# Side-by-side substitution for the latents' triangular inverses in a DeltaNet and PEER kernel

## The chip, the cores and the metric

One core of one Trainium2 chip. The metric is the device time of one execution in microseconds (us); lower is better. Engines: PE (TensorE), DVE (VectorE), ACT (ScalarE), POOL (GpSimd), SP (which here only issues DMAs).

## The reference, cut to what matters

One DeltaNet layer over 512 latent tokens, seeded by scans over 256 context tokens, then a PEER expert layer. The part that the change touches is the inverse of a unit lower-triangular matrix per chunk, head and direction:

```python
def _unit_lower_inverse(a):
    """(I + a)^-1 for strictly lower-triangular a (..., C, C), C = 2^DN_CHUNK_LOG2."""
    eye = jnp.eye(a.shape[-1], dtype=a.dtype)
    t = eye - a
    p = a
    for _ in range(DN_CHUNK_LOG2 - 1):
        p = p @ p
        t = t @ (eye + p)
    return t
...
    a = jnp.where(strict, jnp.einsum('bhnid,bhnjd->bhnij', kb, k) * dmat, 0.0)
    t = _unit_lower_inverse(a)
    u = t @ (v * beta[..., None])
    w = t @ (kb * jnp.exp(G)[..., None])
```

The kernel works with chunks of 128 tokens instead of 64, which gives the same scan. The latents then have 4 chunks x 8 heads = 32 matrices of 128 x 128 for each of two directions (the set N[0], in the trace Nf, is upper-triangular in memory, the set N[1], Nb, lower). The context has 32 matrices for both directions together (Nc).

## The kernel before

**Rounds.** `Trunk.run` is written as rounds t = 1 to 50 (the loop `for t in range(1, nj + 3)`). Round t does one step of several jobs: the projection of job t (`Pj`, 24 matmuls of 512 columns, L333, into one of two PSUM buffers "pz"), the convolution taps of job t-1 (one ACT copy, L346, and four dependent DVE instructions, L353, which free the pz), copies to tokens for job t-2 (L758), the split of the weight block for job t+2 into a high part on ACT (L325) and a low part "wl" on POOL (L326), and the load of a weight block on SP's queue. Jobs 0 to 31 are the context's and the latents' q and k; jobs 32 to 47 are alternately values ("v") and gates ("g") in the order `vgvvgggvvgvggvvg`. A gate job has no taps: its pz is freed by ACT. Two raw weight blocks and three split ones are held at a time.

**The inverse.** A set of 32 matrices is inverted in blocks of 32 x 32: `inv_blocks` copies the diagonal blocks together (L433), transposes them on DVE (L445, L447), clears the result V on POOL (L451 to L453), and then runs 31 steps of forward substitution. Step p is, for each set, a multiplication (L459) of column p of A with row p of V into a scratch tile invT, and a subtraction (L462) of that from the rows below p. Each has (31-p)(p+1) elements per partition. Both run on DVE: `PI` and `PS`, which could send some to POOL, are empty. For the latents the two sets alternate: multiply set 0, multiply set 1, subtract set 0, subtract set 1, so that neighbours never depend on each other. For the context there is one set, and each instruction needs the one before. `inv_merge` then transposes and copies on DVE (L473, L433) and joins the blocks by small matmuls (L487) with ACT copies between them (L501 to L539).

**What orders the work.** The inverses are Python generators; `fill` advances one by so many yields at fixed places of a round. The latents' generator starts at the end of round 33 (one yield), gets four yields in each of rounds 34 to 48, and what is left in round 49. The two constants `SL = (50, 2)` are its last round and the steps per slice: after every two steps `inv_blocks` yields twice. The set-up takes 10 yields, the 31 steps 30, and the merges of both sets 32. The program order so made is a priority: the instruction order on each engine is fixed at build time from it and from when operands are expected to be ready, and an engine then runs its list strictly in order. In rounds 41 to 48, DVE also has four multiplications per round with the adaLN weights (L203, tile adaw).

**Memory.** Each of the latents' sets has a work tile of 4096 floats per partition (A, V, and UT, whose start serves as Cc for the first copies): set 0 in pool `tp` (tag big), set 1 in pool `ux`, whose space was the context's until its scans ended. invT is 256 floats with two buffers.

After the rounds, the latents' scan (L550, L558 and others) needs both inverted sets, and everything behind it (output projection, queries, experts) follows the scan.

Of the kernel before, what the change touches and what calls it, by code (L numbers as in the profile page):

```python
# [9 lines left out]
F32 = mybir.dt.float32  # L10
# [5 lines left out]
OP = mybir.AluOpType  # L16
# [4 lines left out]
P = 128  # L21
# [41 lines left out]
MODS = ((25, 2, 0, 8), (41, 4, 16, 8))  # L63
MO = (48, 64)
SC = (17, 28, 2)
SL = (50, 2)
SCAN0 = 25
HOLD = 3
MK = (6, 2)
# [10 lines left out]
HP = dict(taps=0, silu=0, split=0, copies=0, c=0, l=0)  # L80
ALD = "aAaAaaAaAaaAAAaA"
WOV = (3, 4, 5, 6)
PI = (0, 0)
PS = (0, 0)
CONSTS = ("ident", "le", "ge", "ones", "iota", "half")
CONSTS_R = ("gt", "lt", "ident", "negf", "negb")

# [24 lines left out]
class Trunk:  # L112
# [308 lines left out]

    def inv_work(self, N, nf, pool):
        ws = pool.tile([P, 4096], F32, name="inv", tag="big", bufs=1)
        A, V = (ws[:, i * 1024:(i + 1) * 1024].rearrange("p (a b) -> p a b", b=32) for i in range(2))
        UT = ws[:, 2048:4096].rearrange("p (k x) -> p k x", x=64)
        Cc = ws[:, 2048:3072].rearrange("p (x k) -> p x k", k=32)
        return N, nf, A, V, UT, Cc, self.tp.tile([P, 256], F32, name="invT", bufs=2)

    def cp(self, i, nf, b, dst, src):
        nc, e = self.nc, CP[i][nf // 16][b]
        nc.scalar.copy(dst, src) if e == "a" else (nc.vector if e == "v" else nc.gpsimd).tensor_copy(dst, src)  # L433

    def inv_blocks(self, sets, per):
        nc, half = self.nc, self.C["half"]
        swap = lambda z: z.rearrange("p i x -> p x i")
        for N, nf, A, V, UT, Cc, T_ in sets:
            for b in range(4):
                r = blk(b)  # L440
                self.cp(0, nf, b, Cc[r], N[r, :, r].rearrange("p k x -> p x k"))
                if len(sets) > 1:
                    yield
            if nf:
                nc.vector.transpose(A, Cc)  # L445
            if nf < 32:
                nc.vector.transpose(swap(V if nf else A), Cc)  # L447
            if 0 < nf < 32:
                nc.vector.tensor_scalar(A, A, half[:, 0:1], None, op0=OP.mult)
                nc.vector.scalar_tensor_tensor(A, V, half[:, 1:2], A, op0=OP.mult, op1=OP.add)  # L450
            nc.gpsimd.memset(V, 0.0)  # L451
            nc.gpsimd.memset(V.rearrange("p a b -> p (a b)")[:, 0:1024:33], 1.0)
            nc.gpsimd.memset(UT, 0.0)  # L453
            yield
        for p in range(31):
            n = 31 - p
            ms = [T_[:, :n * (p + 1)].rearrange("p (j c) -> p j c", c=p + 1) for *_, T_ in sets]
            for i, (m, (N, nf, A, V, *_)) in enumerate(zip(ms, sets)):
                (nc.gpsimd if i and PI[0] <= p < PI[1] else nc.vector).tensor_tensor(m, A[:, p + 1:, p:p + 1].to_broadcast([P, n, p + 1]),  # L459
                                        V[:, p:p + 1, :p + 1].to_broadcast([P, n, p + 1]), op=OP.mult)  # L460
            for i, (m, (N, nf, A, V, *_)) in enumerate(zip(ms, sets)):
                (nc.gpsimd if i and PS[0] <= p < PS[1] else nc.vector).tensor_tensor(V[:, p + 1:, :p + 1], V[:, p + 1:, :p + 1], m, op=OP.subtract)  # L462
            if p % per == per - 1:
                yield
                yield

    def inv_merge(self, N, nf, A, V, UT, Cc, T_):
        nc = self.nc
        W = A
        swap = lambda z: z.rearrange("p i x -> p x i")  # L470
# [46 lines left out]
        for l2 in (0, 16):  # L517
            W2s, ps = [], []
            for lo in (l2, l2 + 8):
                s, d = (0, 1) if up(lo) else (1, 0)  # L520
# [82 lines left out]
    def run(self):  # L603
        nc, a, C, mod, ng, dram, tc = self.nc, self.a, self.C, self.mod, self.ng, self.dram, self.tc
        with ExitStack() as tk:
# [247 lines left out]
            mq, mk, live, sums, sqs = [], [], [], [], []  # L853

            def inv_c():
                w = self.inv_work(Nc, 16, self.tp)
                yield from self.inv_blocks([w], SC[2])
                yield from self.inv_merge(*w)

            def inv_l():  # L860
                w = [self.inv_work(N[0], 32, self.tp), self.inv_work(N[1], 0, ux)]
                yield from self.inv_blocks(w, SL[1])
                g = [self.inv_merge(*x) for x in w]
                while g:
                    u = g.pop(0)
# [899 lines left out]
```

## Time and profile before

| what | us |
|---|---|
| median of 3 runs | 1951.41 |
| lowest and highest run | 1949.15, 1956.68 |
| time of the profiled execution | 1956.64 |
| its span in the profile | 1954.9 |
| PE busy | 1819.3 (93%) |
| DVE busy | 1562.8 (80%) |
| POOL busy | 625.6 (32%) |

All trace rows come from the one profiled execution; the time around its span is 1956.64 - 1954.9 = 1.74 us. A timeline row gives start and duration in us; where an instruction had to wait after it was issued, its duration includes the wait, and the bracket at the end says how long the engine was idle before it and for whom.

### The profile page before, as it was taken

What the parts mean: (1) busy time and instruction counts of PE and PEld (TensorE: products, weight loads), DVE (VectorE), ACT (ScalarE), POOL (GpSimd) and SP (SyncE); (2) the same over time, 40 slices, a digit from 0 to 9 for tenths busy, and PEclk for the clock granted to TensorE, in tenths of its full rate; (3) what the DMA queues carried; (4) which work ended last, traced back from release to release, by engine and by line L of the source; (5) the groups of instructions that cost most, each with busy time, mean ns of one, the idle gap of its engine ahead of it and who ended that gap; (6) DMA issues with size and microseconds to landing.
All of it is one profiled execution on the core that took longest, in us unless ns stands there. A gap on an engine that the chain in (4) does not pass through costs nothing.

```text
span 1954.9 us, 29971 instructions
## 1 busy us (share of the span) xinstructions
PE 1819.3 (93%) x11119; PEld 1609.9 (82%) x11119; DVE 1562.8 (80%) x3267; ACT 855.1 (44%) x1399; POOL 625.6 (32%) x395
## 2 busy tenths in 40 slices
PE   7778899878998899799999999999999999999997
PEld 4776788766898887689999888788999998889996
DVE  5998967979388789978999687777777887777885
ACT  3655634523445243247666533333333333333333
POOL 1544412361001133321111022333444443434433
PEclk8888879988799899899999999999999999999998
DMA  8221346424635532147999989999989988989981
GB/s 307 67 87 54 87 130 207 133 86 146 190 114 179 177 98 87 55 162 265 308 316 316 327 292 321 323 346 323 314 311 326 334 304 311 328 304 318 325 275 64
DMA packets 202274, 440.65 MB, mean 225 GB/s; under 512 B 15504, under 2 KB 103696, under 8 KB 198800
## 3 DMA queue, kind: packets, MB, share of 16 engines
q1 hardware_dynamic: 155472, 269.87, 42.5%
q0 software_dynamic: 36864, 134.23, 19.4%
q10 hardware_dynamic: 9792, 34.64, 4.4%
q8 instruction: 87, 1.43, 0.3%
q14 instruction: 59, 0.48, 0.1%
HBM read 388.88 MB, written 49.81 MB: 224 GB/s over the span
## 4 chain that ended last, share of the span: by engine, by line
PE 51%; DVE 11%; DMA 5%; issue 1%; SPq 1%; ACT 0%; DVEq 0%; ACTq 0%
PE pz L1232 25%; PE y L1574 21%; PE py L1509 2%; DMA hTt<-hT_d 2%; DMA ge<-pre_d 2%; DVE wk L1350 1%; PE pz L333 1%; DVE keys L1353 1%; DVE keys L1352 1%; DVE row L1288 1%; DVE keys L1349 1%; DVE keys L1351 1%; DVE wl L1603 1%; DMA keys<-G_d 0%; PE pk L1106 0%
## 5 line engine op out<-in xcount | busy, mean ns | idle before, releaser
L1232 PE MATMUL pz<-hH,wh 128*128 128x384 f32 (+1 forms) x1128 | 391.6, 347 | 2.5 <-ACT small L1253 2.5
L1232 PE MATMUL pz<-hH,wl 128*128 128x384 f32 (+1 forms) x1128 | 389.2, 345 | 0.0
L1232 PE MATMUL pz<-hL,wh 128*128 128x384 f32 (+1 forms) x1128 | 388.8, 345 | 0.0
L1280 POOL DMA_INDIRECT row<-u,small x128 | 169.0, 1320 | 478.3 <-DVE row L1288 456.1
L1597 ACT CAST wh<-w 128x1024 fp32r<-128x1024 f32 x196 | 205.4, 1054 | 181.7 <-PE y L1574 98.0
L1603 DVE TENSOR_TENSOR wl<-w,wh 128x1024 fp32r<-128x1024 f32 x196 | 240.4, 1227 | 46.5 <-ACT wh L1597 46.3
L1280 POOL DMA_INDIRECT row<-v,small x128 | 180.2, 1408 | 223.1 <-DVE small L1296 204.8
L326 POOL TENSOR_TENSOR wl<-w,wh 128x1024 fp32r<-128x1024 f32 x53 | 149.0, 2814 | 294.6 <-ACT wh L325 291.2
L1574 PE MATMUL y<-wh,ch 128*128 128x512 f32 x768 | 238.6, 392 | 2.8 <-ACT ch L1560 2.8
L1574 PE MATMUL y<-wh,cl 128*128 128x512 f32 x768 | 238.0, 391 | 1.8 <-DVE cl L1561 1.8
L1574 PE MATMUL y<-wl,ch 128*128 128x512 f32 x768 | 237.7, 391 | 0.0
L1232 PEld LDWEIGHTS pz<-hH,wh 128*128 128x128 f32 x1128 | 213.6, 189 | 9.5 <-ACT small L1253 2.9
L1232 PEld LDWEIGHTS pz<-hL,wh 128*128 128x128 f32 x1128 | 213.4, 189 | 6.4 <-issue 0.2
L1232 PEld LDWEIGHTS pz<-hH,wl 128*128 128x128 f32 x1128 | 213.2, 189 | 4.3
L1574 PEld LDWEIGHTS y<-wh,cl 128*128 128x128 f32 x768 | 144.2, 188 | 33.4 <-DVE cl L1561 2.8
L1574 PEld LDWEIGHTS y<-wl,ch 128*128 128x128 f32 x768 | 144.5, 188 | 31.4
L1574 PEld LDWEIGHTS y<-wh,ch 128*128 128x128 f32 x768 | 143.5, 188 | 28.9 <-ACT ch L1560 3.5
L1296 DVE SCALAR_TENSOR_TENSOR small<-row,small 128x1024 f32<-128x1024 f32 x127 | 162.6, 1280 | 1.2
L1288 DVE SCALAR_TENSOR_TENSOR row<-row,small 128x1024 f32<-128x1024 f32 x128 | 155.2, 1219 | 0.0
L1253 ACT ACTIVATE ge<-pz 128x384 f32<-128x384 f32 x108 | 53.5, 495 | 214.1 <-PE pz L1232 212.8
L333 PE MATMUL pz<-hlH,wh 128*128 128x512 f32 x256 | 112.4, 439 | 24.4 <-DVE acc L353 19.8
L1516 ACT ACTIVATE keys<-py 128x512 f32<-128x512 f32 x96 | 105.0, 1093 | 55.7 <-PE py L1509 50.8
(477 smaller groups left out, 3361.0 us busy)
## 6 DMA issues: line engine op xcount, KB each, us to landing
w<-uT SPq DMA_DIRECT2D x128, 512.0 KB, 5.0
w<-v SPq DMA_DIRECT2D x128, 512.0 KB, 5.1
w<-w_in SPq DMA_DIRECT2D x48, 512.0 KB, 3.7
G_d<-keys ACTq DMA_DIRECT2D x24, 1024.0 KB, 6.5
adaw<-adaT SPq DMA_DIRECT2D x64, 256.0 KB, 3.4
keys<-G_d SPq DMA_DIRECT2D x8, 1536.0 KB, 13.5
Gt<-G_d SPq DMA_DIRECT2D x8, 1536.0 KB, 13.8
w<-w_q SPq DMA_DIRECT2D x16, 512.0 KB, 3.7
```

Of the source, the lines that this page charges most:

```text
L326: self.last_split = (eng or nc.gpsimd).tensor_tensor(wl, w, wh.bitcast(F32), op=OP.subtract)
L333: self.nc.tensor.matmul(z[:, :T], w_[c // 4][:, c % 4, :] if isinstance(w_, list) else w_[:, c, :], src[x_][:, c, :], start=c + n == 0, st ...
L1232: self.nc.tensor.matmul(out, w[i][:, c, :], x_[:, c, sl], start=c == 0 and n == 0, stop=c == NC - 1 and n == 2)
L1253: self.nc.scalar.activation(ge, z, AF.Gelu)
L1280: nc.gpsimd.indirect_dma_start(out=r, out_offset=None, in_=a["u"] if k < P else a["v"], in_offset=bass.IndirectOffsetOnAxis(ap=self.idx[:, ...
L1288: nc.vector.scalar_tensor_tensor(r, r, 1.0, self.xg, op0=OP.mult, op1=OP.mult, accum_out=self.hid_g[:, k:k + 1])
L1296: nc.vector.scalar_tensor_tensor(self.yg, r, self.coef[:, k:k + 1], self.yg, op0=OP.mult, op1=OP.add)
L1509: nc.tensor.matmul(gp[:, r * P:(r + 1) * P], e[:, 2 + r // 2, :, r % 2], oa[:, 2 * w + r // 2, :, r % 2], start=r == 0 and w == 0, stop=w ...
L1516: nc.scalar.activation(Gs[:, :, i * 4:i * 4 + 4].rearrange("p a t -> p t a"), gps.pop(p).rearrange("p (t a) -> p t a", t=4), AF.Copy, scal ...
L1574: nc.tensor.matmul(yp[2 * t + hf], c_[:, t * P:(t + 1) * P], v_[:, hf * 512:hf * 512 + 512], start=b == 0 and w == 0, stop=b == NBLK - 1 a ...
L1597: nc.scalar.copy(wh, w)
L1603: nc.vector.tensor_tensor(wl, w, wh.bitcast(F32), op=OP.subtract)
```

## The change

The two sets of the latents get one common tile for A and V (in pool `ux`), arranged so that A of set 0 and A of set 1 lie one behind the other, and so do the two V; both UT share the tile in `tp`. One multiplication and one subtraction per step then cover both sets, with twice the elements: 62 instructions for the 31 steps in place of 124. invT becomes one buffer of 2 x 256. The context's inverse goes through the same code with one set. A slice has three steps in place of two, so the 31 steps take 20 yields in place of 30. The constants `PI` and `PS`, which chose no step, go.

```diff
--- before.py
+++ after.py
@@ -63,7 +63,7 @@
 MODS = ((25, 2, 0, 8), (41, 4, 16, 8))
 MO = (48, 64)
 SC = (17, 28, 2)
-SL = (50, 2)
+SL = (50, 3)
 SCAN0 = 25
 HOLD = 3
 MK = (6, 2)
@@ -80,8 +80,6 @@
 HP = dict(taps=0, silu=0, split=0, copies=0, c=0, l=0)
 ALD = "aAaAaaAaAaaAAAaA"
 WOV = (3, 4, 5, 6)
-PI = (0, 0)
-PS = (0, 0)
 CONSTS = ("ident", "le", "ge", "ones", "iota", "half")
 CONSTS_R = ("gt", "lt", "ident", "negf", "negb")
 
@@ -421,21 +419,25 @@
 
 
 
-    def inv_work(self, N, nf, pool):
-        ws = pool.tile([P, 4096], F32, name="inv", tag="big", bufs=1)
-        A, V = (ws[:, i * 1024:(i + 1) * 1024].rearrange("p (a b) -> p a b", b=32) for i in range(2))
-        UT = ws[:, 2048:4096].rearrange("p (k x) -> p k x", x=64)
-        Cc = ws[:, 2048:3072].rearrange("p (x k) -> p x k", k=32)
-        return N, nf, A, V, UT, Cc, self.tp.tile([P, 256], F32, name="invT", bufs=2)
+    def inv_work(self, sets, av, uts):
+        n = len(sets)
+        AV = av[:, :2048 * n].rearrange("p (q s a b) -> p q s a b", q=2, s=n, b=32)
+        T_ = self.tp.tile([P, 2, 256], F32, name="invT", bufs=1)[:, :n]
+        w = []
+        for i, (N, nf) in enumerate(sets):
+            ut = uts[:, i * 2048:i * 2048 + 2048]
+            w.append((N, nf, AV[:, 0, i], AV[:, 1, i], ut.rearrange("p (k x) -> p k x", x=64),
+                      ut[:, :1024].rearrange("p (x k) -> p x k", k=32)))
+        return w, AV[:, 0], AV[:, 1], T_
 
     def cp(self, i, nf, b, dst, src):
         nc, e = self.nc, CP[i][nf // 16][b]
         nc.scalar.copy(dst, src) if e == "a" else (nc.vector if e == "v" else nc.gpsimd).tensor_copy(dst, src)
 
-    def inv_blocks(self, sets, per):
+    def inv_blocks(self, sets, As, Vs, T_, per):
         nc, half = self.nc, self.C["half"]
         swap = lambda z: z.rearrange("p i x -> p x i")
-        for N, nf, A, V, UT, Cc, T_ in sets:
+        for N, nf, A, V, UT, Cc in sets:
             for b in range(4):
                 r = blk(b)
                 self.cp(0, nf, b, Cc[r], N[r, :, r].rearrange("p k x -> p x k"))
@@ -454,17 +456,15 @@
             yield
         for p in range(31):
             n = 31 - p
-            ms = [T_[:, :n * (p + 1)].rearrange("p (j c) -> p j c", c=p + 1) for *_, T_ in sets]
-            for i, (m, (N, nf, A, V, *_)) in enumerate(zip(ms, sets)):
-                (nc.gpsimd if i and PI[0] <= p < PI[1] else nc.vector).tensor_tensor(m, A[:, p + 1:, p:p + 1].to_broadcast([P, n, p + 1]),
-                                        V[:, p:p + 1, :p + 1].to_broadcast([P, n, p + 1]), op=OP.mult)
-            for i, (m, (N, nf, A, V, *_)) in enumerate(zip(ms, sets)):
-                (nc.gpsimd if i and PS[0] <= p < PS[1] else nc.vector).tensor_tensor(V[:, p + 1:, :p + 1], V[:, p + 1:, :p + 1], m, op=OP.subtract)
+            sh = [P, len(sets), n, p + 1]
+            m = T_[:, :, :n * (p + 1)].rearrange("p s (j c) -> p s j c", c=p + 1)
+            nc.vector.tensor_tensor(m, As[:, :, p + 1:, p:p + 1].to_broadcast(sh), Vs[:, :, p:p + 1, :p + 1].to_broadcast(sh), op=OP.mult)
+            nc.vector.tensor_tensor(Vs[:, :, p + 1:, :p + 1], Vs[:, :, p + 1:, :p + 1], m, op=OP.subtract)
             if p % per == per - 1:
                 yield
                 yield
 
-    def inv_merge(self, N, nf, A, V, UT, Cc, T_):
+    def inv_merge(self, N, nf, A, V, UT, Cc):
         nc = self.nc
         W = A
         swap = lambda z: z.rearrange("p i x -> p x i")
@@ -853,13 +853,15 @@
             mq, mk, live, sums, sqs = [], [], [], [], []
 
             def inv_c():
-                w = self.inv_work(Nc, 16, self.tp)
-                yield from self.inv_blocks([w], SC[2])
-                yield from self.inv_merge(*w)
+                ws_ = self.tp.tile([P, 4096], F32, name="inv", tag="big", bufs=1)
+                w, *av = self.inv_work([(Nc, 16)], ws_[:, :2048], ws_[:, 2048:])
+                yield from self.inv_blocks(w, *av, SC[2])
+                yield from self.inv_merge(*w[0])
 
             def inv_l():
-                w = [self.inv_work(N[0], 32, self.tp), self.inv_work(N[1], 0, ux)]
-                yield from self.inv_blocks(w, SL[1])
+                w, *av = self.inv_work([(N[0], 32), (N[1], 0)], ux.tile([P, 4096], F32, name="invA", bufs=1),
+                                       self.tp.tile([P, 4096], F32, name="inv", tag="big", bufs=1))
+                yield from self.inv_blocks(w, *av, SL[1])
                 g = [self.inv_merge(*x) for x in w]
                 while g:
                     u = g.pop(0)
```

## Rows read from the trace of the kernel before

**Rows 1.** The page, busy time and share of each engine
```profile
PE 1819.3 (93%) x11119; PEld 1609.9 (82%) x11119; DVE 1562.8 (80%) x3267; ACT 855.1 (44%) x1399; POOL 625.6 (32%) x395
```

**Rows 2.** Stretches of 20 us; busy us and count per engine, granted clock, DMA share
```profile
400.00:420.00 20.00, 11.06 (x42) 8.67 (x41) 14.19 (x44) 1.55 (x2) 18.71 (x2) 0.79 0.12 25
...
440.00:460.00 20.00, 12.16 (x53) 9.77 (x51) 19.91 (x48) 4.94 (x9) 4.90 (x3) 0.82 0.53 167
...
480.00:500.00 20.00, 20.00 (x334) 16.69 (x333) 11.39 (x25) 9.13 (x15) 4.70 (x2) 0.83 0.45 146
...
500.00:520.00 20.00, 20.00 (x235) 17.53 (x232) 3.59 (x9) 10.41 (x22) 2.35 (x1) 0.74 0.38 107
```

**Rows 3.** Timeline of PE, latents' stage: start, duration, line, operation [idle before]
```profile
416.44 0.79 PE L333 MATMUL pz<-hlH,wl 128*128 128x512 f32 x1 [8.94 <-POOL wl L326]
...
430.61 0.47 PE L333 MATMUL pz<-hlH,wh 128*128 128x512 f32 x1 [0.87 <-DVE acc L353]
...
438.18 0.47 PE L333 MATMUL pz<-hlH,wh 128*128 128x512 f32 x1 [1.38 <-DVE acc L353]
...
457.64 0.77 PE L333 MATMUL pz<-hlH,wh 128*128 128x512 f32 x1 [7.84 <-DVE acc L353]
...
530.84 5.61 PE L550 MATMUL pk<-S,kT 128*128 128x128 f32 x32
```

**Rows 4.** Timeline of POOL, latents' stage
```profile
370.41 0.95 POOL L451 MEMSET inv<- 128x1024 f32 x1
...
396.65 19.73 POOL L326 TENSOR_TENSOR wl<-w,wh 128x1024 fp32r<-128x1024 f32 x1 [6.39 <-ACT wh L325]
...
422.03 2.40 POOL L326 TENSOR_TENSOR wl<-w,wh 128x1024 fp32r<-128x1024 f32 x1 [3.33 <-ACT wh L325]
```

**Rows 5.** Timeline of DVE, latents' stage; a row of x2 starts both within it
```profile
380.77 1.25 DVE L445 STREAM_TRANSPOSE inv<-inv 128x1024 f32<-128x1024 f32 x1 [2.26 <-ACT inv L433]
...
392.59 0.40 DVE L459 TENSOR_TENSOR invT<-inv 128x87 f32<-128x87 f32 x2
...
392.91 0.40 DVE L462 TENSOR_TENSOR inv<-inv,invT 128x87 f32<-128x87 f32 x2
...
406.60 0.76 DVE L459 TENSOR_TENSOR invT<-inv 128x256 f32<-128x256 f32 x2
...
407.27 0.76 DVE L462 TENSOR_TENSOR inv<-inv,invT 128x256 f32<-128x256 f32 x2
...
413.79 0.40 DVE L462 TENSOR_TENSOR inv<-inv,invT 128x231 f32<-128x231 f32 x1
...
425.83 0.74 DVE L353 SCALAR_TENSOR_TENSOR acc<-pz,cw,acc 128x504 f32<-128x504 f32 x1 [11.64 <-ACT acc L346]
...
433.31 1.90 DVE L462 TENSOR_TENSOR inv<-inv,invT 128x192 f32<-128x192 f32 x1
...
435.79 0.34 DVE L462 TENSOR_TENSOR inv<-inv,invT 128x192 f32<-128x192 f32 x1
...
450.10 0.73 DVE L353 SCALAR_TENSOR_TENSOR acc<-pz,cw,acc 128x504 f32<-128x504 f32 x1
...
460.26 2.12 DVE L473 STREAM_TRANSPOSE inv<-inv 128x1024 f32<-128x1024 f32 x1
...
462.86 2.83 DVE L433 COPY inv<-inv 32x1024 f32<-32x1024 f32 x4
```

**Rows 6.** Timeline of DVE, context's stage (one set)
```profile
191.37 0.31 DVE L462 TENSOR_TENSOR inv<-inv,invT 128x156 f32<-128x156 f32 x1
...
191.71 1.07 DVE L459 TENSOR_TENSOR invT<-inv 128x175 f32<-128x175 f32 x1
...
222.64 0.42 DVE L459 TENSOR_TENSOR invT<-inv 128x252 f32<-128x252 f32 x1
...
223.09 0.42 DVE L462 TENSOR_TENSOR inv<-inv,invT 128x252 f32<-128x252 f32 x1
```

**Rows 7.** Timeline of POOL, context's stage
```profile
191.53 1.06 POOL L382 TENSOR_TENSOR rw<-cbuf,gH 128x512 fp32r<-128x512 f32 x1 [0.63 <-PE aux L399]
```

## The prediction

> **What bounds the kernel now.** First the engines' totals: PE is busy for 1819.3 us of the span, DVE for 1562.8 [rows 1]. That is a mean over unlike stages, so next come the stretches of 20 us of the stage that the change touches: there PE falls to 11 or 12 us in 20, and is full again from 480 us on [rows 2]. So PE waits first, and is the bound after it. PE's timeline says for what: 8.94 us for a split on POOL, then three times for the taps on DVE, 0.87, 1.38 and 7.84 us [rows 3]; together 19.0 us. POOL's row behind the first is the striking one: a split that takes 2.40 us elsewhere took 19.73 us, and ended at 416.38 us, just before PE went on [rows 4]. In those 19.73 us DVE ran substitution steps without a gap, from 392.59 us to 413.79 + 0.40 = 414.19 us, and then stood idle for 11.64 us, as the starved split had held up PE and with it the next taps [rows 5]. So DVE's row of substitutions starved POOL, POOL starved PE, PE then starved DVE.
>
> **What the change does to an instruction.** Start-to-start, two instructions of 87 elements take 0.32 us (392.59 to 392.91), two of 256 elements 0.67 us (406.60 to 407.27) [rows 5]. The slope is (0.335 - 0.16) / (256 - 87) = 1.036 ns per element, the fixed part 0.335 - 0.265 = 0.070 us. These neighbours are independent. In the context's single set each needs the one before: 252 elements take 0.45 us start to start, a fixed part of 0.45 - 0.261 = 0.189 us [rows 6]. After the change the latents are such a chain. Per step: before 4 x 0.070 = 0.28 us plus the elements, after 2 x 0.189 = 0.38 us plus the same elements. Half the instructions therefore cost DVE 0.10 us **more** per step, 2.8 us over steps 1 to 29, which stand ahead of the taps of job 42. Between chained instructions DVE can slip in something else: eight taps and six L203 stand there now, each hiding about 0.189 - 0.070 = 0.12 us, 1.7 us in all; net +1.1 us. Bounds: were merged pairs as well overlapped as now, 29 x (0.14 - 0.28) = -4.1 us; were each to restart for its second set, 29 x (4 x 0.189 - 0.28) = +13.8 us. I take the chain's value, as it is the same code with one set.
>
> The durations bear on a rule. One 256-element instruction shows 0.76 - 0.335 = 0.425 us, of which 0.16 us is not slope, but only 0.070 us of that is paid between independent neighbours [rows 5]. The Trainium skill, VectorE: DVE Perf Modes, section The DRAIN you can't avoid, says that the next operation does not start until the pipeline empties, and its rules ask to minimise the count of operations; its errata section gives (N+151)/0.96 ns. By that each saved instruction is worth some 157 ns, an estimate from that page, and the sum would be 9.7 us lower. The trace agrees on the duration and not on the pitch; the rule is a rival below.
>
> **What it does to POOL.** Between chained instructions DVE shows a gap: in the context's stage one ends at 191.37 + 0.31 = 191.68 us, the next starts at 191.71 us but takes 1.07 us [rows 6]. POOL had issued an operation at 191.53 us and it ran its 1.06 us undisturbed [rows 7]: POOL got in at the gap, and DVE waited. So I expect the 19.73 us to fall to about 2.4 us and PE's 8.94 us to go. It is not free: each split that falls among substitutions now holds DVE up. The 192-element subtraction that met one took 1.90 us in place of 0.34 us [rows 5], so 1.56 us, at most the split's 2.40 us; I take 2.0. The splits of jobs 39 to 41, of which the first was starved and the next two ran while DVE was idle, now fall among steps: 3 x 2.0 = +6.0 us on DVE (4.7 to 7.2).
>
> **What it does to the order.** The generator shrinks from 10 + 30 + 32 = 72 yields to 62, so merges stand 2.5 rounds earlier in priority, ahead of some L203. Their DVE part is about 2 x 2.1 + 2 x 2.8 = 9.8 us per set (transposes and copies) [rows 5]. I cost the shift at nothing: from 457.64 us to the scan's first matmul at 530.84 us PE has no wait as long as those, and is busy for 20.00 us in 20 from 480 to 520 [rows 2, 3], so joins that are ready sooner only change places with projections. If that cover is gone, PE waits for transposes in the middle of a projection; that is the rival on the slow side.
>
> **Smaller edits.** V of set 0 now lies in the space that the context's scans give up; its clear on POOL ran at 370.41 us and would wait a few us, while its first reader, the transpose at 380.77 us, waits for ACT's copies anyway [rows 4, 5]: nothing, at most 2.3 us. One invT buffer: chained instructions never need two. No DMA is added; SP's weight load behind the starved split is freed earlier. New waits: each subtraction needs the multiplication ahead of it; behind it on DVE stand taps, which PE waits for, and they can use the gap.
>
> **The sum.** DVE paces the stage up to the taps of job 42, begun at 450.10 us [rows 5], which let PE go on at 457.64 us. On DVE's path the idle time goes, -11.64; the chain adds +1.1; the splits add +6.0: -4.5 us. PE's run behind that is unchanged and passes it on. The profiled execution, 1956.64 us, would be 1952.1; it stands 5.23 us above the median 1951.41, so the median becomes **1946.9 us**. Ends of this case: -11.64 - 4.1 + 4.7 = -11.0 and -11.64 + 13.8 + 7.2 + 2.3 = +11.7.
>
> **The rivals.** A measurement of this kernel can tell about 0.5% from no change, 9.8 us.
> (a) *PE's waits go altogether.* If the taps are slipped into the gaps of the chain as soon as they are ready, PE no longer waits for DVE: 19.0 us, and the matmuls at the lower granted clock behind each long wait (0.79 in the stretch with the longest, that is partly at 1.2 GHz [rows 2]) come back too, a few us. For it: context taps do alternate with steps. Against it: DVE is busy 19.91 us in 20 just ahead of 457 us, so work must be done before. Half to all: -10 to -22 us, about 1935. Chance 0.20.
> (b) *The fixed part is saved after all.* Each instruction pays its 0.16 us, 62 x 0.16 = -9.9 us in place of +1.1: -4.5 - 11.0 = -15.5 us, 1936. This is the page's rule above; the pitch in [rows 5, 6] speaks against it. Chance 0.10.
> (c) *POOL stays starved.* Then the change does not do its main part: no idle time goes, and DVE has +1.1 us: 1952.5. The Trainium skill bears on it too: SBUF — State Buffer, section Who interferes with whom, says that a DVE instruction with two SBUF inputs contends with a POOL one that reads SBUF and that the second blocks until the first has finished. The trace shows POOL blocked across 57 DVE instructions, not one [rows 4, 5]. By the page alone DVE would not be the cause of the 19.73 us, and it would stay. Chance 0.06.
> (d) *Slower: merges ahead of taps.* If the transposes and copies of both sets (2 x 9.8 = 19.6 us) stand ahead of the taps of job 42 on DVE, those come 19.6 - 7.3 (what the taps and the merge work among them took, 450.10 to 457.4) - 4.5 = 7.8 us later, PE's list holds job 44 ahead of the joins and waits, and its clock falls once more: +8 to +14 us, 1963. It decides at one point: whether job 42's taps are ready at build time before step 30 is done. For it: the merges stand two and a half rounds earlier. Against: the chain's gaps let taps through. Chance 0.16.
>
> **How the numbers follow.** My case has the remaining 0.48. Faster by over 0.5%: (a), (b) and a small tail, 0.32. Within: my case and (c), 0.52. Slower: most of (d), 0.16. The range reaches into (a) and (b) on one side and (d) on the other: 1931 to 1961, leaving about 0.1 on each side; my case's own is 1940 to 1953.
>
> **What the profile would show.** Right: 62 substitution instructions of double size with gaps of 0.03 us; no POOL split over 5 us; some double-size steps of 2 to 3 us where a split got in; DVE's 11.64 us idle gone; PE's wait for POOL gone but waits for the taps still there, job 44 begun about 453 us and the scan at about 526. Wrong: a split of over 10 us on POOL (c); PE nearly full from 388 us (a); a stall of over 10 us ahead of job 44 with transposes on DVE (d).

## The result, and the profile after

The change made the kernel slower: 1976.54 us, median of four runs, against 1950.80 us; the ratio is 1.0134, 95% interval 1.0097 to 1.0171, or +25.7 us. 1946.9 was forecast, and the range ended at 1961. The profiled execution of the changed kernel has a span of 1973.5 us (before: 1954.9). Line numbers moved by one or two: L461 and L462 are now the substitution's multiplication and subtraction, L201 the modulation product (the multiplication with the adaLN weights, L203 before), L331 the projections, L487 the joins; pk is the PSUM bank that the joins and the scan write.

**VectorE and POOL did what was forecast.** POOL's timeline in the latents' stage, start and duration, answers to [rows 4]:

```profile
396.21 2.85 POOL L324 TENSOR_TENSOR wl<-w,wh 128x1024 fp32r<-128x1024 f32 x1 [6.53 <-ACT wh L323]
402.13 2.63 POOL L324 TENSOR_TENSOR wl<-w,wh 128x1024 fp32r<-128x1024 f32 x1 [3.06 <-ACT wh L323]
```

The split that took 19.73 us takes 2.85 us. VectorE's timeline, which answers to [rows 5]:

```profile
392.38 0.68 DVE L201 SCALAR_TENSOR_TENSOR adaw<-adaw,cb 128x512 f32<-128x512 f32 x1
...
402.54 2.64 DVE L461 TENSOR_TENSOR invT<-invA 128x384 f32<-128x384 f32 x1
...
418.88 2.30 DVE L203 TENSOR_TENSOR mod<-mod,adab 128x8 f32<-128x8 f32 x1
...
422.52 0.68 DVE L462 TENSOR_TENSOR invA<-invA,invT 128x504 f32<-128x504 f32 x1
423.24 0.69 DVE L461 TENSOR_TENSOR invT<-invA 128x510 f32<-128x510 f32 x1
...
451.58 0.72 DVE L351 SCALAR_TENSOR_TENSOR acc<-pz,cw,acc 128x496 f32<-128x496 f32 x1
...
454.71 0.22 DVE L462 TENSOR_TENSOR invA<-invA,invT 128x62 f32<-128x62 f32 x1
```

Three more rows of VectorE in the kernel before, to set beside these:

```profile
436.70 0.68 DVE L203 SCALAR_TENSOR_TENSOR adaw<-adaw,cb 128x512 f32<-128x512 f32 x1
...
453.85 1.90 DVE L473 STREAM_TRANSPOSE inv<-inv 128x1024 f32<-128x1024 f32 x1
...
456.20 0.66 DVE L433 COPY Nf<-inv 32x1024 f32<-32x1024 f32 x1
```

Chained neighbours stand 423.24 - 422.52 = 0.72 us apart; the forecast's 0.189 + 504 x 1.036 ns gives 0.71. A step that meets a split (402.54) is held for some 2 us. New is L201 at 392.38: a modulation product in a gap of the chain, 44 us earlier than the first of its lot in the kernel before (436.70). TensorE's waits from 380 to 470 us, first of the kernel before, then of the changed one (engine, what waited, for whom; total us, times, longest):

```profile
PE pz L333 <- DVE acc L353: 18.7, 4, 8.6
PE pz L333 <- POOL wl L326: 8.9, 1, 8.9
```
```profile
PE pz L331 <- DVE acc L351: 24.6, 3, 11.7
PE pk L487 <- DVE inv L435: 3.2, 1, 3.2
```

27.6 us of waiting became 27.8 (the wait that ends at some 388 us, 8.6 and 8.5 us, is in both; the prediction's 19.0 us leave it out): POOL's wait is gone, longer waits for VectorE's taps and a new one of the joins stand in its place. Still, job 44 starts earlier. TensorE's timeline of the changed kernel, which answers to [rows 3]:

```profile
452.45 0.74 PE L331 MATMUL pz<-hlH,wh 128*128 128x512 f32 x1 [4.41 <-DVE acc L351]
...
467.75 2.25 PE L487 MATMUL pk<-inv,Nf 32*32 32x32 f32 x61 [3.21 <-DVE inv L435]
...
474.65 0.80 PE L331 MATMUL pz<-hlL,wh 128*128 128x512 f32 x1
475.24 0.63 PE L331 MATMUL pz<-hlH,wl 128*128 128x512 f32 x1
475.80 4.59 PE L487 MATMUL pk<-inv,Nb 32*32 32x32 f32 x93
...
535.24 0.63 PE L331 MATMUL pz<-hlH,wl 128*128 128x512 f32 x1
535.67 0.63 PE L331 MATMUL pz<-hlH,wh 128*128 128x512 f32 x1
...
538.05 0.40 PE L331 MATMUL pz<-hlH,wh 128*128 128x512 f32 x1
538.28 0.40 PE L331 MATMUL pz<-hlL,wh 128*128 128x512 f32 x1
...
548.38 1.86 PE L550 MATMUL pk<-S,kT 128*128 128x128 f32 x7
```

Job 44 at 452.45 us is 5.2 us ahead of before. The scan, 73.20 us behind job 44 before, now comes 95.93 us behind it: 17.5 us late.

**Where it went: TensorE's clock.** Stretches of the changed kernel (columns as in [rows 2]; the number behind POOL's count is the granted clock):

```profile
440.00:460.00 20.00, 15.60 (x64) 12.54 (x63) 19.47 (x27) 4.94 (x9) 4.95 (x3) 0.91 0.36 106
460.00:480.00 20.00, 16.79 (x273) 14.95 (x272) 15.77 (x17) 4.43 (x7) 2.58 (x1) 0.74 0.13 41
480.00:500.00 20.00, 20.00 (x285) 17.30 (x283) 4.30 (x8) 8.00 (x13) 2.35 (x1) 0.50 0.17 54
500.00:520.00 20.00, 20.00 (x219) 17.55 (x215) 0.00 (x0) 4.46 (x8) 0.00 (x0) 0.50 0.01 2
520.00:540.00 20.00, 20.00 (x111) 16.25 (x111) 9.57 (x19) 6.89 (x14) 2.35 (x1) 0.55 0.40 132
540.00:560.00 20.00, 15.80 (x146) 14.59 (x145) 9.32 (x32) 6.63 (x13) 2.36 (x1) 0.79 0.84 258
```

Before, the clock was 0.83 and 0.74 from 480 to 520 us [rows 2]. Now 0.50, that is 1.2 GHz: projections stand 0.43 us apart at 535.24, and 0.23 us once the clock is back (538.05). The stretch from job 44 to the scan as one row each, before and after:

```profile
457.64:530.84 73.20, 72.13 (x1005) 62.64 (x1005) 40.17 (x79) 31.93 (x59) 9.42 (x4) 0.80 0.49 150
```
```profile
452.45:548.38 95.93, 92.04 (x1004) 78.90 (x1004) 38.66 (x59) 32.03 (x59) 9.63 (x4) 0.62 0.23 74
...
470.95:536.00 65.05, 65.05 (x755) 56.32 (x753) 17.49 (x30) 22.24 (x39) 4.69 (x2) 0.50 0.14 45
```

Busy time times clock is 72.13 x 0.80 = 57.7 us before and 92.04 x 0.62 = 57.1 us after: the same work, at another clock. From 470.95 to 536.00 us TensorE was busy for all of 65.05 us and stayed at 1.2 GHz. What it did there stands in the program's order (P projections, j joins of 32 x 32, the small ones, J joins of 64 x 64, the large ones, S the scan; the trace has two rows for each join; the first three projections of job 44 before, the first six after, are left out):

```
before  P21 j64 P16 j64 P8 j16 P6 j80 P18 j64 P1 j32 P23 J128 S
after   P37 j80 P2 j64 P7 j80 P5 j16 P1 j80 P3 J8 P1 J8 P4 J24 P4 J8 P2 J24 P4 J8 P20 J48 S
```

Joins that are ready sooner cut the projections into pieces of 1 to 7; the clock rose at 538 us, within the one piece of 20. The Trainium skill, TensorE: Matmul & The Clock Gate, section What's actually happening, says that the gate goes by how busy TensorE has been, and lists busy beside 2.4 GHz. This trace has a TensorE without idle time at 1.2 GHz for 65.05 us, so the profile's busy share does not tell the clock.

### The profile page after: what moved, and what is told of

The parts are those of the page before. It is cut to its first block, busy times and chain, and to the rows that moved or that the text cites. A ratio compares the mean times of both kernels' runs of the same rounds, so it can differ in the third digit from the quotient of the medians.

```text
span 1973.5 us, 29906 instructions
## 1 busy us (share of the span) xinstructions
PE 1836.8 (93%) x11119; PEld 1624.6 (82%) x11119; DVE 1570.4 (80%) x3205; ACT 855.7 (43%) x1399; POOL 607.8 (31%) x395
## 4 chain that ended last, share of the span: by engine, by line
PE 67%; DVE 24%; DMA 4%; issue 2%; ACT 1%; SPq 1%; POOL 0%; DVEq 0%; ACTq 0%; POOLq 0%
PE pz L1234 26%; PE y L1576 21%; PE pz L331 6%; PE pk L487 4%; PE py L1511 2%; DVE acc L351 2%; DVE invT L461 2%; PE pk L550 2%; DMA ge<-pre_d 1%; DVE invA L462 1%; DVE wk L1352 1%; DVE adaw L201 1%; PE pz L550 1%; DMA hTt<-hT_d 1%; DVE rw L380 1%
## 5 line engine op out<-in xcount | busy, mean ns | idle before, releaser
L324 POOL TENSOR_TENSOR wl<-w,wh 128x1024 fp32r<-128x1024 f32 x53 | 132.4, 2500 | 346.3 <-ACT wh L323 346.3
L331 PE MATMUL pz<-hlH,wh 128*128 128x512 f32 x256 | 112.4, 439 | 32.2 <-DVE acc L351 27.5
```

The source lines that it names most:

```text
L324: self.last_split = (eng or nc.gpsimd).tensor_tensor(wl, w, wh.bitcast(F32), op=OP.subtract)
L331: self.nc.tensor.matmul(z[:, :T], w_[c // 4][:, c % 4, :] if isinstance(w_, list) else w_[:, c, :], src[x_][:, c, :], start=c + n == 0, st ...
```

## The experiments

The clock theory: the list's order, by the clock, is the loss. The rival, the chain theory: the side-by-side chain is late by itself. All ratios are of medians, to the kernel before on the same chip. "Not granted" is the sum of 20 us x (1 - granted clock) over the eight stretches from 440 to 600 us; "chain", "projection" and "scan" are the starts of the last substitution step, the last projection and the scan's last matmul (v times qar), in us, of the one profiled execution. An edge is an order put into the list by hand: `issue_after` keeps an instruction behind a named one.

| kernel | ratio (95%) | not granted | chain | projection | scan |
|---|---|---|---|---|---|
| before | 1 | 18.8 | 453.8 | 512.8 | 604.7 |
| the change | 1.0134 (1.0097 to 1.0171) | 41.0 | 454.7 | 540.6 | 628.2 |
| e1_side_two | 1.0028 (1.0003 to 1.0053) | 29.0 | 464.2 | 520.9 | 614.0 |
| e2_alt_three | 1.0021 (0.9998 to 1.0044) | 20.6 | 443.6 | 527.2 | 613.7 |
| e4_pairs | 0.9983 (0.9963 to 1.0002) | 24.0 | 451.0 | 514.2 | 605.3 |
| e5_adaw_taps | 1.0067 (1.0041 to 1.0092) | 25.6 | 446.6 | 527.0 | 613.5 |
| e6_bulk | 1.0107 (1.0077 to 1.0138) | 37.6 | 457.7 | 486.7 | 622.7 |
| e7_coarse | 1.0040 (1.0012 to 1.0068) | 25.6 | 464.1 | 522.4 | 613.7 |
| e8_gated | 1.0056 (1.0032 to 1.0079) | 27.2 | 462.4 | 524.8 | 617.1 |
| e9_filler | 1.0236 (1.0195 to 1.0276) | 32.2 | 455.1 | 560.7 | 649.6 |
| e10_change_coarse | 1.0069 (1.0042 to 1.0095) | 30.6 | 457.0 | 531.9 | 620.5 |
| e11_two_taps | 1.0006 (0.9986 to 1.0026) | 18.6 | 451.1 | 512.9 | 601.2 |
| e12_two_taps_coarse | 1.0004 (0.9980 to 1.0028) | 23.8 | 450.1 | 513.0 | 604.0 |
| e13_before_coarse | 0.9999 (0.9978 to 1.0020) | 13.8 | 452.8 | 508.8 | 599.8 |
| e14_two_mods_late | 1.0019 (0.9994 to 1.0044) | 17.2 | 440.6 | 503.3 | 600.8 |
| e15_before_mods_late | 1.0043 (1.0020 to 1.0067) | 22.4 | 449.4 | 512.2 | 609.5 |
| e16_forced_pairs | 1.0063 (1.0038 to 1.0089) | 30.8 | 457.2 | 519.8 | 610.8 |
| e17_three_mods_late | 1.0121 (1.0091 to 1.0151) | 32.4 | 435.4 | 520.4 | 619.3 |

Without e9, which adds work, a line through the 17 kernels gives 1.03 us on the scan for each us not granted, correlation 0.90; with the chain's end there is no such order (e17's is the earliest, and it is among the slowest). The last projection's start is a rival: it goes with the scan as closely, 0.92, if e6 is left out too, but e6 has the earliest of all and a late scan. Two cautions: the columns are of one execution each, and e4, whose TensorE list is that of before, has 24.0 where before has 18.8, so a few us of "not granted" tell nothing; and the sum counts TensorE's idle stretches too.

### The halves of the change

**e1_side_two**: the change, `-SL = (50, 3)` `+SL = (50, 2)`.

> Both sets side by side as in the change, but slices of two rows as before. Clock theory (the loss is TensorE's clock at 0.50 from 470 to 536 us, because the list lets the joins in between pieces of 1 to 7 projection matmuls): in this kernel's list 62 projection matmuls stand ahead of the first join, so they run at the high clock; granted clock of 460 to 520 us above 0.7, the scan's first matmul at 525 to 538 us, 1945 to 1958 us in all. Chain theory (the side-by-side steps on VectorE, with POOL's splits and modulation products let into their gaps, are late by themselves): clock as low as or lower than the change's, scan at 545 or later, 1970 us or more.

**e2_alt_three**: the kernel before, `-SL = (50, 2)` `+SL = (50, 3)`.

> The alternating steps of before, but slices of three rows: the other half of the change alone. Clock theory: three-row slices put the joins earlier in the list, in pieces of 2 to 24 projection matmuls, coarser than the change's 1 to 7: granted clock of 460 to 520 us between 0.6 and 0.85, 1948 to 1965 us. Chain theory: nothing of the chain is changed, so the time stays within 0.3% of before, 1945 to 1956 us. Both: POOL's split at about 396 us still takes over 10 us.

Neither half makes the loss: +0.28% and +0.21% against +1.34%. e1's time is where the clock theory put it, its details are not: the clock was 0.50 and 0.52 from 480 to 520 us and the scan began at 540.6. 62 projections ahead of the joins did not help the joins behind them, which had 11 projections among 320. And its chain ended 10 us later than the change's. VectorE's groups from 380 to 470 us, first the change's, then e1's:

```profile
L201 DVE SCALAR_TENSOR_TENSOR adaw<-adaw,cb 128x512 f32<-128x512 f32 x14 | 9.5, 681 | 0.0
```
```profile
L201 DVE SCALAR_TENSOR_TENSOR adaw<-adaw,cb 128x512 f32<-128x512 f32 x26 | 26.2, 1008 | 1.4 <-DMA adaw<-adaT 1.4
```

With two steps a slice, 26 modulation products ran in that stretch in place of 14; a part of the chain theory holds. e2's time does not tell the theories apart.

### The list and the clock

**e10_change_coarse**: the change, with two edges in the list.

```diff
-            nc.tensor.matmul(out[:, (k % per) * w:(k % per) * w + w], l, r_,
+            self.last_join = nc.tensor.matmul(out[:, (k % per) * w:(k % per) * w + w], l, r_,
...
+                joins[t] = getattr(self, 'last_join', None)
                 if 4 <= t < nj:
-                    Pj(t)
+                    with tc.issue_after(joins[t - 0].ins) if t in (46, 47) else ExitStack():
+                        Pj(t)
```

> The changed kernel with one thing altered: jobs 46 and 47 stand behind the joins traced before them, so that from the second piece on TensorE's list is 24 whole projections, 32 large joins, 24 projections, 32, the scan, where the change has pieces of 1 to 7. VectorE's chain up to the joins (470 us) is the change's. Clock theory: the clock is at 0.50 from 470 us until the first piece of 24 and comes back there: 30 to 50 us at 0.50 instead of 70, the scan's last matmuls 8 to 18 us earlier, 1956 to 1968 us. Chain theory (the loss lies before the joins): 1972 us or more.

Half the loss went, 1.34% to 0.69%, with VectorE's order up to the joins untouched (behind them a few taps and modulation products change places). The clock came back earlier:

```profile
480.00:500.00 20.00, 20.00 (x392) 19.19 (x388) 4.36 (x8) 9.74 (x16) 2.36 (x1) 0.50 0.17 56
500.00:520.00 20.00, 19.32 (x177) 17.61 (x174) 2.12 (x7) 6.20 (x13) 0.00 (x0) 0.52 0.17 54
520.00:540.00 20.00, 18.76 (x185) 16.60 (x184) 9.68 (x18) 9.37 (x17) 4.71 (x2) 0.91 0.55 171
```

30.6 us not granted against 41.0, the scan's last matmul 7.7 us earlier (8 to 18 were expected). This is the cleanest case for the clock: the order of the same matmuls alone moved it and the time. The last projection came 8.7 us earlier as well; e6 below shows that this by itself is not it.

**e7_coarse**: e1 with the same two edges. **e8_gated**: with a third, `t in (45, 46, 47)`.

> Both sets side by side, slices of two rows, and two edges in TensorE's list that keep projections whole: jobs 46 and 47 stand behind the joins traced before them. The list becomes 45 projections, 224 small joins, 24 projections, 96 small joins, 24 projections, 128 large joins, the scan. Clock theory: with pieces of 24 the granted clock comes back between the joins; mean of 460 to 520 us 0.75 or more, under 15 us at 0.50, the scan's first matmul at 520 to 533 us, 1938 to 1952 us. Chain theory: what e1 lost lies on VectorE and stays, 1955 us or more. A third outcome, clock high but no gain: TensorE waits for the first joins with projections queued behind them, seen as idle PE over 8 us before 475 us.

> As the one before, with a third edge: job 45 too stands behind the first joins, so the list is 21 projections, 128 small joins, 24, 96, 24, 96, 24, 128 large joins, the scan: nearest to the list of the kernel before. Clock theory: the clock of 470 to 520 us is 0.75 or more, but TensorE stands idle 8 to 14 us before the first joins (they are ready at some 470 us, job 44 ends at some 459 us), so the scan starts 3 to 8 us later than in the run with two edges: 1942 to 1960 us. Chain theory: 1957 us or more with the clock no different from the run with two edges.

A miss: whole jobs did not help e1 (1958.33 and 1961.18 us, above the clock theory's ranges, which end at 1952 and 1960). e7 had 25.6 us not granted against 29.0 and lost it in TensorE's wait for the first joins (5.0 us; e8 10.0 us), which came at 475 us with a chain that ended at 464. The chain's own lateness had to go as well.

**e6_bulk**: the change with `-l=0` `+l=-1000`, the inverses' work last in the list.

> The change with the inverses' work at a lower priority in the list, so that 68 projection matmuls stand ahead of the first join, 24 more among the next 84 joins, and the other 236 small and 128 large joins in one piece with nothing between. Clock theory: the 92 projections run at the high clock (0.23 us each, some 25 us instead of 41), and the scan starts at 520 to 540 us even if the last joins run at the low clock (some 0.049 and 0.12 us each, by the rows of the changed kernel at the low clock): 1943 to 1965 us. If joins alone in one piece hold the high clock, the lower half of that range. Chain theory: not faster than the change, 1970 us or more.

The last projection starts at 486.7 us, and still the time is 1972.99 us, outside the clock theory's range and where the rival put it. The trace speaks for the clock all the same: the joins in one piece ran at 0.50 from 491 us on, and the scan's first 15 us too, 37.6 us not granted in all. What fell is my form of the theory: fine pieces are not what lowers the clock. It fell among the joins, in one piece or in many, and rose again where whole projections ran.

**e9_filler**: the change, with needless matmuls (WARM is 4) into a bank before its joins.

```diff
+        def bank():
+            z = self.pk()
...
+                    for _ in range(WARM):
+                        nc.tensor.matmul(z[:, :512], self.hl[0][:, 0, :P], self.hl[0][:, 0, :], start=True, stop=True)
+            return z
```

> The changed kernel with work added to TensorE alone: 4 needless 128x512 matmuls ahead of the joins of each of the 28 banks, 112 in all, overwritten by the joins; VectorE's and ACT's work is the change's. Clock theory: large matmuls among the joins keep the granted clock up (0.75 or more from 470 to 530 us), so that 112 x 0.21 us = 24 us more work costs nothing or less than nothing: 1960 to 1980 us. If the clock is low for another reason (the idle stretch at 467 us, the number of instructions), it stays at 0.50 and the added work is paid at 0.43 us each, 48 us: 2005 to 2030 us.

Between the two: +20.7 us on the change (1997.24 against 1976.54), less than the 48 us at the low level, more than nothing. The clock rose to 0.59 and 0.67 from 480 to 520 us, fell to 0.50 from 520 to 540, and the list of the real projections moved too; the run settles nothing.

### The modulation products

**e5_adaw_taps**: the change, `-AN = (1,0)` `+AN = (1,1)`, by which each L201 has an edge to the last taps written before it, so that the products are kept out of the chain's gaps ahead of those taps. **e11_two_taps**: the same with `SL = (50, 2)`. **e12_two_taps_coarse**: e11 with the two edges of e10.

> The changed kernel, with the modulation products of VectorE kept behind the last taps traced, as they were not: they can no longer run in the gaps of the chain ahead of job 39's taps. TensorE's list becomes 41 projections, 144 small joins, then pieces of 2, 3, 2, 17, 2, 22, 4, 20, 5 and 19. Chain theory: TensorE's wait of 11.73 us for job 39's taps falls to 2 to 6 us and the time by as much, 1966 to 1972 us. Clock theory: the coarser list counts for more: 20 to 40 us at the low clock instead of 70, 1948 to 1964 us, whatever the wait does.

> Both sets side by side in slices of two rows, with VectorE's modulation products kept behind the last taps, so that none stands in the gaps of the chain. TensorE's list: 38 projections, then small joins with pieces of 2, 3, 3, 12, 12, 1 and 23, then the 128 large joins and the scan. If the two causes found so far are the whole loss (modulation products drawn into the chain delay the joins by 8 to 10 us; fine pieces hold the clock low): chain ends at 446 to 456 us, first join at 458 to 466 us, 10 to 30 us at 0.50, scan starts at 520 to 533 us, 1938 to 1952 us. If side by side costs by itself, by its dependent steps: like the run with two rows alone, 1955 us or more.

> As the one before, with jobs 46 and 47 also whole and behind the joins traced before them (38 projections, 224 small joins with 8 projections among them, 24, 96 joins, 24, 128 large joins, the scan). Clock theory: no lower clock than the one before, the last projection at 500 to 515 us, 1936 to 1952 us. If gating only makes TensorE wait for ACT's copies: 2 to 6 us slower than the one before.

e5's chain ends 8 us earlier than the change's and half the loss goes, which puts it into the clock theory's range; the chain theory's reason did not come, as the wait for the taps hardly fell (11.0 us) and TensorE waited another 12.1 us for the first joins. e11 takes the whole loss away: 1.0006, with 18.6 us not granted, as before. Its order is near that of before: P38 j32 P3 j32 P2 j64 P3 j16 P12 j80 P12 j64 P1 j32 P23 J128. Its TensorE waits, 380 to 470 us:

```profile
PE pz L331 <- DVE acc L351: 19.8, 3, 11.3
PE pk L487 <- DVE inv L435: 2.9, 1, 2.9
```

So side by side with two steps a slice and the products kept out costs nothing against the kernel before, and gives nothing: 22.7 us of waits in place of 27.6, its scan starts at 528.9 us against 530.84. VectorE is the limit there: it is busy for 19.4 to 19.9 us in each 20 from 400 to 460 us. e12 measures as e11, though its profiled execution has 23.8 us not granted against 18.6, where no lower clock was expected. The kernel before with `AN = (1,1)` alone was not run: what keeping the products out is worth there, and so what side by side is worth by itself, is not shown.

### Is there a version that beats both?

**e13_before_coarse**: the kernel before with the two edges. **e14_two_mods_late**: e11 with `-(41, 4, 16, 8)` `+(45, 8, 16, 4)` in MODS (the second lot of products from round 45, eight a round, in place of round 41, four a round). **e15_before_mods_late**: the kernel before with that edit alone. **e17_three_mods_late**: e14 with `SL = (50, 3)`.

> The kernel before, nothing side by side, with jobs 46 and 47 whole and behind the joins traced before them: what the list alone is worth. Clock theory: its pieces of 16 to 23 are already coarse, 1943 to 1955 us, within 0.4% of before. If whole jobs help by themselves, below 1943 us.

> Both sets side by side, slices of two rows, modulation products behind the last taps, and the second lot of them (32) traced four jobs later, 8 a job instead of 4, so that none stands in the chain. TensorE's list: 21 projections, 128 small joins, 24, 96, 24, 96, 24, 128 large joins, the scan. If the products in the chain were what held the joins up: the chain ends at 438 to 446 us (451 in the run with them), the first join at 450 to 456 us, the scan at 512 to 525 us, 1932 to 1946 us. If something else sets the scan's start (the clock, ACT's copies, the taps): joins earlier, time within 0.3% of before, 1943 to 1955 us.

> The kernel before, alternating steps, with the second lot of modulation products traced four jobs later: the control for the run above. By the first theory it gains less than the side-by-side one, as POOL's split is still kept out for some 20 us and TensorE still waits 8 to 9 us for it: 1938 to 1952 us, and POOL's split at 396 us still over 10 us. If it gains as much or more, side by side has nothing of its own to give.

> As the first of these, with slices of three rows, the change's own. TensorE's list: 41 projections, 272 small joins in one piece, 24, 56 joins, then pieces of 2, 22, 4, 20, 5, 19 among the large joins. Clock theory: the piece of 272 small joins runs at 0.50 and the pieces of 20 to 24 bring the clock back: 25 to 40 us at 0.50; the last projection comes behind 80 large joins, so the loads for the scan are late and its first unit waits: 5 to 15 us slower than the first of these, 1944 to 1960 us. If only the chain counts: as fast as the first of these.

None beats the kernel before. e13 measures as before, as the clock theory had it. e14's chain ends at 440.6 us, 13 us earlier than before, and the scan begins at 527.2 (512 to 525 were expected): joins that are ready sooner wait for their place, and TensorE stands 4.8 us for ACT in the last ones. e15 missed its range, 1958.71 us against 1938 to 1952. Of e15 and e14, with the same edit of MODS, the side-by-side one is 0.24% ahead, with intervals that overlap, and it alone has `AN = (1,1)`: that tells nothing of side by side. e17 is the plainest case against the chain theory: the earliest chain of all, 435.4 us, and +1.21% (1972.66 us, over both ranges), with its joins at 0.50 from 460 to 480 us. Its loss is not the clock alone: ahead of the scan and in its first part TensorE stood idle for 6.5 us for ACT's copies and 6.2 us for VectorE.

### What lets POOL in

**e4_pairs**: the kernel before, each set's product and subtraction written next to each other. The order on VectorE came out as that of before but for a few places, so this is nearly a second run of the kernel before (POOL's two splits from 395.48 us took 20.75 us), and tells only how far such runs differ. **e16_forced_pairs** sets the order by edges, with AN = (1,1):

```diff
+                with self.tc.issue_after(self.last_step.ins) if len(sets) > 1 and (p or nf == 0) else ExitStack():
...
+                    self.last_step = nc.vector.tensor_tensor(V[:, p + 1:, :p + 1], V[:, p + 1:, :p + 1], m, op=OP.subtract)
```

> The kernel before, with only the order of VectorE's four instructions of a step changed: one set's product, then its subtraction, which waits for it, then the other set's two; TensorE's list is the same as before. If POOL is let in wherever two neighbours on VectorE depend on each other: no split of POOL over 5 us from 390 to 425 us, TensorE's wait of 8.94 us for POOL gone, VectorE's chain longer by 62 steps x 0.1 = 6 us, 1944 to 1953 us. If it is only the halved count of instructions that freed POOL: the split at 396 us still takes over 10 us, and the wait of 8.94 us stays; 1951 to 1958 us.

> Alternating instructions at single width as before, but by edges in the order product, subtraction of one set, then product, subtraction of the other: each subtraction waits for its neighbour, each product does not. Modulation products behind the last taps, so that the neighbours stay neighbours from 390 to 420 us. If a dependent neighbour lets POOL in: no split over 5 us from 390 to 425 us. If the halved count does it: a split of 10 to 20 us at about 396 us. The time is not the point: TensorE's list has fine pieces (54 projections, then 80 joins, 2, 64, 4, ...), so by the clock theory 1955 to 1970 us.

e16's VectorE, then its POOL:

```profile
397.79 0.38 DVE L460 TENSOR_TENSOR invT<-inv 128x220 f32<-128x220 f32 x1
398.20 2.46 DVE L462 TENSOR_TENSOR inv<-inv,invT 128x220 f32<-128x220 f32 x1
400.59 0.38 DVE L460 TENSOR_TENSOR invT<-inv 128x220 f32<-128x220 f32 x1
```
```profile
397.94 2.48 POOL L326 TENSOR_TENSOR wl<-w,wh 128x1024 fp32r<-128x1024 f32 x1 [3.36 <-ACT wh L325]
403.38 2.51 POOL L326 TENSOR_TENSOR wl<-w,wh 128x1024 fp32r<-128x1024 f32 x1 [2.96 <-ACT wh L325]
```

The split is issued at 397.94, while a single-width product runs; that ends at 398.17, the subtraction behind it starts 0.03 us later and is held, so in that gap the split got in; all five splits from 392 to 417 us took 2.39 to 2.61 us. With as many instructions as before, dependent neighbours suffice: it is not the halved count.

## Why the prediction was wrong

1. **Instruction costs: right.** 0.71 us forecast, 0.72 measured; that each saved instruction is worth its fixed part (rival b) had no support: chained neighbours pay 0.72 us for 504 elements, as in the context's chain.
2. **POOL let in: right**, and by the gap named (e16). The wait of 8.94 us went. Rival (c) did not come.
3. **Splits holding VectorE up: right**, some 2 us each. From 392 to 452 us eight of VectorE's rows are held in this way, five before: three more, as forecast.
4. **Job 44 at about 453 us: right**, 452.45. But in part by luck, as two things that the sum leaves out about cancel. Ahead of job 42's taps there now stood 14 modulation products in place of six, some 5 us more. And these taps ended (451.58 + 0.72 = 452.30) ahead of the last eight substitution instructions, which took until 454.93, where before a transpose and a copy (453.85, 456.20) stood among them: some 5 us less. I counted the gaps as room for taps and for six products already there, and did not ask what else the list would put in.
5. **The step that failed** is "I cost the shift at nothing". Its ground was true, TensorE was busy throughout, and joins did change places with projections. The error was to take a busy engine's time as independent of the order: the same 57 us of work at full clock took 92 us in place of 72. The ten yields' shift of priority (72 to 62) and the products in the chain's gaps together made that order: with three steps a slice and the products kept out (e5) +0.67%, with whole projections (e10) +0.69%, with two steps alone (e1) +0.28%, with two steps and the products kept out (e11) none. These overlap and don't add up.
6. **The slower rival (d)** had the sign and not the place: transposes and copies did not delay job 42's taps. The clock stood in [rows 2] at 0.83 and 0.74 in a stretch where TensorE was never idle; that was the row to ask from.
7. The scan starts 17.5 us late and its last matmul is 23.5 us late (628.2 against 604.7); at the end of the two profiled executions 18.6 us are left (1973.5 against 1954.9). Part of what the scan adds is a wait. VectorE of the changed kernel, then TensorE's wait:

```profile
546.70 0.69 DVE L201 SCALAR_TENSOR_TENSOR adaw<-adaw,cb 128x512 f32<-128x512 f32 x1 [6.10 <-DMA adaw<-adaT]
...
554.31 0.69 DVE L201 SCALAR_TENSOR_TENSOR adaw<-adaw,cb 128x512 f32<-128x512 f32 x1 [0.73 <-DMA adaw<-adaT]
...
555.13 0.60 DVE L558 SCALAR_TENSOR_TENSOR X<-pk,neg_l,vn 128x128 f32<-128x128 f32 x2
```
```profile
PE pk L550 <- DVE X L558: 3.5, 1, 3.5
```

VectorE's first instruction of the scan (L558) stands behind modulation products that wait for their loads, and TensorE waits 3.5 us for it; the clock is 0.79 from 540 to 560 us, 1.00 in the same stretch before. The loads are late with the last projection, which started 28 us later (DMA share 0.01 and 0.40 from 500 to 540 us, before 0.38 from 500 to 520 [rows 2]); that earlier loads would save the wait is argued from these rows, not tried.

What stays open is what in the joins lowers the clock. The rows narrow it. Stretches of e5, then of e6:

```profile
500.00:520.00 20.00, 20.00 (x179) 16.68 (x177) 8.20 (x17) 9.17 (x15) 4.30 (x2) 1.00 0.53 171
```
```profile
520.00:540.00 20.00, 17.49 (x166) 16.91 (x164) 6.46 (x19) 6.62 (x13) 0.00 (x0) 0.50 0.43 132
```

In e5 the large joins ran there between pieces of 2 to 22 projections, and the clock stayed high; so it did in the kernel before from 512 to 524 us (1.00), behind 23 projections in one piece. In e6 they ran behind small joins that had run at 0.50, and it stayed low. So large joins need not lower a high clock, and did not raise a low one; in the kernel before the falls without a wait ahead came in or right behind small joins (at 470, 480, 490 and 500 us). It is no rule: in e13 the clock fell to 0.50 among the last large joins (522.3 to 526 us), in e17 at 490 us. Why some joins lower it and others do not is not shown. Also open is why e13, with 5 us more clock granted in its profiled execution, measures the same as before; that execution took 1943.23 us, 6 us under the median of its runs, and that of before 1956.64 us, 6 us over its own.

## What to carry to other kernels

A matmul engine that is busy throughout still has a time that hangs on the order of its list: read the granted clock of each stretch beside its busy share, and multiply the two before you call a reordering free. When a chain of instructions becomes dependent, ask what the list and the other engines will put into its gaps: here POOL's splits (wanted) and modulation products (not wanted). A change of slicing is a change of every engine's list: test it apart from the arithmetic.

## What was unexpected of the hardware

TensorE without an idle moment stayed at 1.2 GHz for 65.05 us, over 755 rows of matmuls, most of them joins of 32 or 64 columns; a projection took 0.43 us there and 0.23 us later. POOL was kept out for 19.73 us while VectorE's neighbours were independent of each other, and got in at gaps of 0.03 us between dependent ones. Even an addition of 128 x 8 took 2.30 us on VectorE when a split had got in ahead of it (418.88 us; 0.16 us for its like at 421.69).
